# A two-layer hybrid block on one core: the second layer's input projection as seven half-size products, with keys, values and gates formed beside the query up-projection

## The chip, the cores and the metric

The kernel runs on one core of one Trainium2 chip, as one launch. The metric is the device time of that launch in microseconds (us); a time is the median of several runs, and runs of one kernel agree within a few tenths of a per cent. TensorE multiplies matrices out of SBUF into PSUM (eight banks), VectorE (DVE) and ScalarE (ACT) read PSUM and SBUF, GpSimd (POOL) works on SBUF alone, and SyncE (SP) mostly issues transfers. Each engine works through its own queue in order.

## The reference, cut to what matters

Two layers work on 2048 tokens (`x`) and 256 context tokens (`ctx`), all with 1024 channels. Each layer normalises and modulates the tokens, multiplies them by an input matrix, mixes, and multiplies by an output matrix. The second layer is the odd mixer:

```
h = rms_norm(x, pre_norm_w) * (1 + sc_x) + sh_x        # h_c likewise from ctx
ckv, kr, mk, mv, mg, cq, mq, mo, z = split_cols(h @ w_in, O_COLS)   # 1024 x 3632
parts_c = split_cols(h_c @ w_in[:, :O_CTX_COLS], O_COLS[:5])        # first 1072 columns
k_x, v_x = mla_keys_values(ckv, kr, ...)      # rms_norm(ckv) @ w_ukv (256 x 1024), rope
q_x = mla_queries(cq, ...)                    # rms_norm(cq) @ w_uq  (768 x 768), rope
c_out = dense_attention_blocks(q_x, [k_c, k_x], [v_c, v_x])
m_out = readout of two mLSTM passes over mq, mk, mv with gates mg
out = (concat(c_out, m_out) * silu(z)) @ w_out
```

All is float32. The kernel keeps that precision by splitting every matmul operand into a rounded part `hi` and a rest `lo` and adding three products: hi·hi, hi·lo, lo·hi.

## The kernel before

The work is written with a tile framework: the program gives operations in an order, the framework allots buffers from pools, orders each engine's queue (mainly by the program's order, but an operation whose inputs are not ready can be passed by a later one), and inserts the waits. A pool's `bufs` is the number of buffers of a tag; a new tile waits until an old one of the tag is free.

There are 18 token tiles of 128; 0 and 1 are the context. Layer 0 ends with its output projection (`out_proj`), which writes the new tokens to `x1_d` in DRAM. Then comes `layer1_in`, which is what the change rewrites. It handles the tokens in three blocks of six tiles:

- `hT_steps` brings a block's tokens in: per pair of tiles a step `norm` loads the rows (L204), squares and sums them on ACT (L207), gets the factor on POOL (L192, L193) and scales on DVE (L209). Four steps `tr` transpose two chunks of 128 channels each on TensorE, apply the modulation on ACT into `hf` (L226) and split on DVE into `hi` (L228) and `lo` (L229).
- `load_w` brings in some 264 or 256 columns of the weight matrix (L252) and splits them: `whi` on ACT (L255), `wlo` half on POOL and half on DVE (L256).
- `block(b, hi, lo)` runs over the columns. Token-major columns (all but `mq` and `z`) take the tokens as stationary operand and up to 264 weight columns as moving one, 24 matmuls (8 channel chunks x 3) into one PSUM bank `acc`, which DVE (L780) or ACT (L783, Sigmoid) reads. Context tiles leave out the columns past 1072. Feature-major columns (`mq`, `z`) take weights as stationary and 384 tokens (512 in block 0) as moving operand; ACT reads the bank (L799, L803). The results go by SP to `p1_d`, `mo_d`, `mqT_d` and `zT_d` in DRAM.
- `alongside` and `run_part` spread other steps over the steps of `block`: over block 0 the tokens of block 1, over block 1 those of block 2.
- Block 2 has two companions. Over its first 54 steps run `kv_steps`: load and normalise `ckv` (L860, L862), rotate the key part, transpose (`tpc`), split (L832, L833), value and key products (`accv`, `acck`, tag `kacc`, two banks) and their stores. Over the next 20 steps run `gates`, which turns the gate columns into the decay tables of the mLSTM with long scans on DVE (L1275, L1279), and the early steps of `uq_steps` (the query weights).

Then `up` runs the rest of `uq_steps`: per tile load and normalise `cq` (L973), transpose, split `cqh`/`cql`, the rotary product `accr` and the other product `accn` (tag `O`, two banks), and stores. The attention follows.

## Time and profile before

| what | value |
|---|---|
| runs | 3470.11, 3472.04, 3472.26 us (median 3472.04) |
| profiled execution, first to last instruction | 3470.3 us |
| mean granted TensorE clock | 0.985 |
| projection of layer 1, first to last `acc` matmul | 1279 to 2042 us |
| query up-projection after it | to some 2172 us |

The results list no separate time for the profiled execution beside its span. The page gives the busy time of each engine; a weight load (PEld) overlaps the matmul before it, and the end of a matmul is modelled, so the busy time of single matmuls overlaps. In groups of instructions the columns are line, engine, operation, output and inputs, shape and count, then busy time and the mean of one in ns, then the idle time of the engine just before them and what ended it. A row of the waits reads: who, for whom, us in total, times, longest. A row of the timeline or of the chain begins with the time from the start of the span and the duration. A row of the stretches names busy time and (x) the number of instructions per engine, then the granted clock, the share of DMA and GB/s.

### The profile page before, as it was taken

To read this page: it belongs to the slowest core of one execution; us is meant where nothing else is said; L and a number is where in the kernel's file an instruction comes from. 1 tells how busy PE (TensorE), PEld (TensorE's weight loads), DVE (VectorE), ACT (ScalarE), POOL (GpSimd) and SP (SyncE) were. 2 spreads that over 40 slices of the span, in tenths; PEclk is the share of its full clock that TensorE was granted. 3 is DMA by queue.
4 is the path that set the end of the run, shared out by engine and by line. 5 is a ranking of instruction groups with operands and counts; after the bars stand their busy time and mean duration, and the time that the engine had idled before them with its cause. 6 is when DMAs were issued, how large, how long until landed. Compare 5 with 4: busy or idle time off the path is not lost.

```text
span 3470.3 us, 57718 instructions
## 1 busy us (share of the span) xinstructions
PE 3385.0 (98%) x21756; PEld 2976.4 (86%) x21756; DVE 1966.5 (57%) x3550; ACT 1692.7 (49%) x3559; POOL 1193.9 (34%) x1451
## 2 busy tenths in 40 slices
PE   7999999999999989999999999999999999998999
PEld 5989999987888869899999989788888888886776
DVE  4443443337777753333243434788888888875555
ACT  4222221136666652312222333677777777776554
POOL 3324133234333331211232234544444444454221
PEclk9999999999999989999999999999999999998999
DMA  7334223442222143434355555451222122015563
GB/s 264 111 107 127 73 79 118 128 139 85 69 83 72 56 150 125 155 121 131 104 168 162 167 155 155 135 101 36 50 62 49 35 51 62 22 34 151 176 179 97
DMA packets 331895, 376.99 MB, mean 109 GB/s; under 512 B 20205, under 2 KB 284441, under 8 KB 327705
## 3 DMA queue, kind: packets, MB, share of 16 engines
q1 hardware_dynamic: 319312, 315.83, 29.8%
q0 software_dynamic: 11888, 56.92, 6.3%
q8 instruction: 172, 2.82, 0.3%
q14 instruction: 107, 0.87, 0.1%
q10 hardware_dynamic: 416, 0.56, 0.1%
HBM read 267.47 MB, written 105.77 MB: 108 GB/s over the span
## 4 chain that ended last, share of the span: by engine, by line
PE 44%; DVE 2%; DMA 1%; issue 1%; ACT 1%; POOL 1%; SPq 0%; DVEq 0%; POOLq 0%; ACTq 0%
PE S L40 12%; PE O L40 8%; PE T L50 7%; PE acc L40 5%; PE Y L40 5%; PE accn L40 2%; PE pa L40 1%; PE pb L40 1%; PE accr L40 1%; PE acck L40 1%; PE accv L40 1%; DMA cq<-p_d 0%; PE cps L40 0%; PE st L40 0%; DVE mx L1099 0%
## 5 line engine op out<-in xcount | busy, mean ns | idle before, releaser
L40 PE MATMUL acc<-h,whi 128*128 128x384 f32 (+2 forms) x2720 | 708.9, 344 | 3.2 <-ACT whi L255 2.2
L40 PE MATMUL acc<-whi,h 128*128 128x256 f32 (+2 forms) x3328 | 618.1, 285 | 0.0
L40 PEld LDWEIGHTS acc<-whi,h 128*128 128x128 f32 x3328 | 522.4, 190 | 5.6 <-issue 3.5
L40 PEld LDWEIGHTS acc<-h,whi 128*128 128x128 f32 x2720 | 487.4, 190 | 43.0 <-issue 6.0
L40 PE MATMUL S<-kt,qt 96*128 96x512 f32 (+1 forms) x2304 | 494.1, 343 | 2.6 <-ACT P L1101 2.3
L1119 POOL TENSOR_SCALAR P<-P,fa 128x768 f32<-128x768 f32 x384 | 340.2, 905 | 431.9 <-ACT ph L1137 372.7
L40 PEld LDWEIGHTS S<-kt,qt 96*128 96x128 f32 x2304 | 400.6, 189 | 91.7 <-ACT P L1101 17.5
L1138 DVE TENSOR_TENSOR pl<-T,ph 128x512 fp32r<-128x512 f32 x576 | 396.1, 688 | 140.5 <-ACT ph L1137 136.8
L40 PE MATMUL acc<-wlo,h 128*128 128x264 f32 (+1 forms) x1664 | 471.3, 283 | 0.4 <-POOL wlo L256 0.4
L40 PE MATMUL acc<-h,wlo 128*128 128x384 f32 (+2 forms) x1360 | 464.4, 342 | 0.6 <-POOL wlo L256 0.4
L1137 ACT ACTIVATE ph<-T 128x512 fp32r<-128x512 f32 x576 | 342.0, 595 | 163.6 <-PE T L50 156.6
L256 POOL TENSOR_TENSOR wlo<-wraw,whi 128x1024 fp32r<-128x1024 f32 (+2 forms) x86 | 204.3, 2375 | 613.2 <-ACT whi L255 597.0
L1099 DVE TENSOR_REDUCE mx<-S 128x1 f32<-128x768 f32 x384 | 365.6, 952 | 42.5 <-PE S L40 29.3
L1101 ACT ACTIVATE P<-S,mx 128x768 f32<-128x768 f32 x384 | 346.0, 901 | 37.6 <-DVE mx L1099 19.3
L255 ACT ACTIVATE whi<-wraw 128x1024 fp32r<-128x1024 f32 (+2 forms) x172 | 168.0, 1009 | 398.5 <-PE acc L40 213.8
L50 PE MATMUL T<-ident,P 128*128 128x128 f32 x2304 | 348.9, 273 | 5.0 <-DVE pl L1138 3.1
L40 PEld LDWEIGHTS acc<-wlo,h 128*128 128x128 f32 x1664 | 316.7, 190 | 1.5 <-POOL wlo L256 0.8
L50 PEld LDWEIGHTS T<-ident,P 128*128 128x128 f32 x2304 | 275.1, 141 | 42.7 <-DVE pl L1138 7.4
L40 PE MATMUL O<-ph,vh 128*128 128x512 f32 x576 | 267.7, 465 | 0.3 <-ACT ph L1137 0.3
L40 PEld LDWEIGHTS acc<-h,wlo 128*128 128x128 f32 x1360 | 257.7, 189 | 11.1 <-POOL wlo L256 0.7
L40 PE MATMUL O<-pl,vh 128*128 128x512 f32 x576 | 238.9, 415 | 0.4 <-DVE pl L1138 0.2
L256 DVE TENSOR_TENSOR wlo<-wraw,whi 128x1024 fp32r<-128x1024 f32 (+2 forms) x86 | 169.5, 1971 | 111.4 <-ACT whi L255 104.9
(406 smaller groups left out, 5783.1 us busy)
## 6 DMA issues: line engine op xcount, KB each, us to landing
wraw<-in_e_w_in_dram SPq DMA_DIRECT2D x48, 512.0 KB, 4.1
mw<-in_mod_w_dram SPq DMA_DIRECT2D x40, 512.0 KB, 3.9
wraw<-in_o_w_in_dram SPq DMA_DIRECT2D x19, 1024.0 KB, 5.2
wraw<-in_o_w_in_dram SPq DMA_DIRECT2D x18, 1056.0 KB, 7.0
wraw<-in_e_w_in_dram SPq DMA_DIRECT2D x15, 1024.0 KB, 5.4
p_d<-o SPq DMA_DIRECT2D x104, 132.0 KB, 2.2
x_d<-y SPq DMA_DIRECT2D x18, 512.0 KB, 2.8
hx<-x_d SPq DMA_DIRECT2D x18, 512.0 KB, 4.1
```

What stands on the lines that cost most here:

```text
L40: T.matmul(o, l, r, start=start, stop=stop)
L50: T.matmul(o, src, idn, is_transpose=True, start=True, stop=True)
L255: A.activation(hi[:, k : k + 4, :n], raw[:, k : k + 4, :n], AF.Copy)
L256: (V if k else G).tensor_sub(lo[:, k : k + 4, :n], raw[:, k : k + 4, :n], f32(hi[:, k : k + 4, :n]))
L1099: V.tensor_reduce(mx, ps, AX.X, ALU.max, negate=True)
L1101: A.activation(P, ps, AF.Exp, bias=mx, accum_out=st["den"][:, j, i : i + 1])
L1119: G.tensor_scalar(P, P, fa[:, j, i : i + 1], 1.0, op0=ALU.mult, op1=ALU.mult)
L1137: A.activation(ph, tp, AF.Copy)
L1138: V.tensor_sub(pl, tp, f32(ph))
```

## The change

The input projection of layer 1 is computed by Winograd's form of Strassen's scheme. For each block the six token tiles are two halves of three tiles (A1, A2), the 1024 channels two halves of four chunks, and the weight columns of a chunk two halves. Seven products of half the tokens, half the channels and half the columns, each again in three terms of hi and lo, replace eight:

- A sums on POOL (`hW_parts`): of the staged tokens `a11, a12, a21, a22` the operands are a11, a12, s1-a11, s1, a12-(s1-a11), a11-a21, a22, with s1 = a21+a22; all seven are split and kept for the whole block.
- B sums on POOL (`wW_parts`): four subtractions for each chunk, and seven splits (hi on ACT, lo now always on DVE), two products ahead of their use.
- The products are added up in PSUM where two follow one another on the same bank (products 1, 4 and 6 continue 0, 3 and 5), and in SBUF by ACT (product 0) and DVE (products 2 to 6).
- The tokens are first staged in float32 (`hW_stage`, two row buffers `hx` in place of four, no split), since the sums need whole blocks; block b+1 is staged beside block b, and its operands are formed in the last chunk of block b.
- Chunks are now 2 x 268, 2 x 320 (token-major), 2 x 128 and 2 x 256 (feature-major) columns, the four PSUM banks `acc` become six, and context columns reach exactly to 1072.
- `kv_steps` and `gates` leave block 2 (only the key weights and two loads stay there). They now run in `up`, merged with the first 40 and the next steps of `uq_steps`, and share the banks `T` and `O` with it.

The rest of the diff takes out comments. Its core:

```diff
+    def hW_stage(l, tiles, stg, xsrc, xp, pp, nx):
+        st = {}
+        def norm(a):
...
+        def tr(a, k):
+            def f():
+                js = [1 if t < 2 else 0 for t in tiles[a : a + 2]]
...
+                for kk in range(2):
+                    d = k + kk
+                    for i, n in ((0, 2),) if js[0] == js[1] else ((0, 1), (1, 1)):
+                        A.activation(stg[:, d, (a + i) * 128 : (a + i + n) * 128], tp[:, kk, i * 128 : (i + n) * 128],
+                                     AF.Identity, bias=B_col[l][:, d, js[i] : js[i] + 1],
+                                     scale=A_col[l][:, d, js[i] : js[i] + 1])
+            return f
...
+    def hW_parts(stg, T, hp, xp):
+        a11, a12 = (stg[:, k : k + 4, :T] for k in (0, 4))
+        a21, a22 = (stg[:, k : k + 4, T:] for k in (0, 4))
+        ops, st = {}, {}
+        two = lambda ap, j: ap[:, 2 * j : 2 * j + 2, :]
...
+                src = (a11, a12, a11, None, a12, a21, a22)[i]
+                for j in range(2):
+                    if i == 2:
+                        s1 = xp.tile([128, 2, 384], F32, tag="hs1", name="hs1", bufs=1)[:, :, :T]
+                        G.tensor_add(s1, two(a21, j), two(a22, j))
+                        G.tensor_sub(two(a21, j), two(a11, j), two(a21, j))
+                        G.tensor_sub(two(a11, j), s1, two(a11, j))
+                        split(*(two(o, j) for o in ops[3]), s1, V)
+                    if i == 4:
+                        G.tensor_sub(two(a12, j), two(a12, j), two(a11, j))
+                    split(*(two(o, j) for o in ops[i]), two(src, j), V)
...
+    def wW_parts(wsrc, halves, n, wp, wmax):
...
+        def part(i):
+            def f():
+                (b11, b21), (b12, b22) = ((raw[j][:, :4, :n], raw[j][:, 4:, :n]) for j in range(2))
+                hi, lo = ops[i] = [wp.tile([128, 4, wmax], F32R, tag=t, name=t, bufs=3)[:, :, :n] for t in ("whi", "wlo")]
+                if i == 2:
+                    st[0], st[1] = (wp.tile([128, 4, wmax], F32, tag="wt", name="wt", bufs=2)[:, :, :n] for _ in range(2))
+                    G.tensor_sub(st[0], b12, b11)
+                    G.tensor_sub(st[1], b22, st[0])
+                if i == 5:
+                    G.tensor_sub(b12, b22, b12)
+                if i == 6:
+                    G.tensor_sub(b21, b21, st[1])
+                split(hi, lo, (b11, b21, st.get(1), st.get(0), b22, b12, b21)[i], V)
+            return f
...
+    def mmW(ps, lhs, rhs, start):
+        for k in range(4):
+            for a, (i, j) in enumerate(((0, 0), (0, 1), (1, 0))):
+                T.matmul(ps, lhs(i, k), rhs(j, k), start=start and k == 0 and a == 0, stop=k == 3 and a == 2,
+                         skip_group_check=True)
...
     def layer1_in(ue):
...
+            halves = [([2, 3, 0], [4, 5, 1]), ([6, 7, 8], [9, 10, 11]), ([12, 13, 14], [15, 16, 17])]
+            chunks = [
+                ([[(0, 268)], [(268, 268)]], True, True),
+                ([[(536, 268)], [(804, 268)]], True, True),
+                ([[(1072, 320)], [(1392, 320)]], True, False),
+                ([[(1712, 128), (2096, 192)], [(2288, 320)]], True, False),
+                ([[(1840, 128)], [(1968, 128)]], False, False),
+                ([[(2608, 256)], [(2864, 256)]], False, False),
+                ([[(3120, 256)], [(3376, 256)]], False, False),
+            ]
...
+                    if more:
+                        start((c + 1) % len(chunks))
+                    lat = 2 if b == 0 else 3
+                    N = n if tm else lat * 128
+                    subs = (3 if both else lat) if tm else n // 128
...
+                    for i in range(NP):
+                        if i + 2 < NP:
+                            parts[i + 2]()
+                            if i + 2 == NP - 1 and more:
+                                ahead[0][1][1]()
+                        elif more:
+                            ahead[0][2][i + 2 - NP]()
+                        h, w = hops[i], wops[i]
+                        for u in range(subs):
+                            us = slice(u * 128, (u + 1) * 128)
+                            cont = i in (1, 4, 6)
+                            if not cont:
+                                ps[u] = pp.tile([128, 512], F32, tag="acc", name="acc", bufs=6)[:, :N]
...
+                            mmW(ps[u], *((hs, ws) if tm else (ws, hs)), not cont)
+                            if i == 0:
+                                m[u] = op.tile([128, 384], F32, tag="m", name="m", bufs=3)[:, :N]
+                                A.activation(m[u], ps[u], AF.Copy)
+                            elif i == 1:
+                                store(new(), *args(0, 0), ps=ps[u])
+                            elif i == 2:
+                                V.tensor_tensor(m[u], ps[u], m[u], op=ALU.add)
+                            elif i == 3:
+                                o22[u] = op.tile([128, 384], F32, tag="v", name="v", bufs=3)
+                                V.tensor_tensor(o22[u][:, :N], ps[u], m[u], op=ALU.add)
...
+                            yield
+                        if nxt and last and i:
+                            nxt[i - 1]()
...
+                alongside(block(0, h0, mk), flat(steps), 85)
+                steps, h2, mk = stage(2)
+                alongside(block(1, h1, mk), flat(steps), 95)
+            gen = block(2, h2, None)
...
+            first, kv = kv_steps(kw, xk)
+            run_part(gen, 119, [lambda: None] * 8 + first)
+            drain(gen)
...
     def up(ue, ks, xk, kv):
...
+        early, pools, us = uq_steps(uw, xk, uc)
...
+        M = 40
+        merge(kv(kp, pp), [lambda: None] * 4 + early + us[:M])
+        ks.close()
         ha = hd_a.enter_context(tc.tile_pool(name="d_a", bufs=1, **tl))
+        first, ld = load_head(0, ha)
+        n = len(ld) - 6
+        with tc.tile_pool(name="u_g", bufs=1, **tl) as q:
+            merge(steps_of(gates(q, pp), 24), us[M:-24])
+        for o, i in ld[:n]:
+            G.dma_start(o, i)
```

More of the change, by code (lines that the diff above doesn't have):

```diff
@@ new lines, in hW_parts, with new, f @@
+    def hW_parts(stg, T, hp, xp):
[3 more added lines that the diff above has]
+        two = lambda ap, j: ap[:, 2 * j : 2 * j + 2, :]
+        def new(i):
+            ops[i] = [hp.tile([128, 4, T], F32R, tag=f"h{i}{j}", name=f"h{i}{j}", bufs=1) for j in range(2)]
+        def part(i):
+            def f():
+                if i == 2:
+                    new(2)
+                    new(3)
+                elif i != 3:
+                    new(i)
+                if i == 3:
+                    return
+                src = (a11, a12, a11, None, a12, a21, a22)[i]
[9 more added lines that the diff above has]
+                    split(*(two(o, j) for o in ops[i]), two(src, j), V)
+            return f
+        return ops, [part(i) for i in range(NP)]
@@ new lines, in layer1_in, with start, block @@
+            ahead = []
+            def start(c):
+                cols = chunks[c][0]
+                ahead.append(wW_parts(w_in, cols, sum(m for _, m in cols[0]), wp, WM))
+                ahead[-1][1][0]()
+            def block(b, hops, nxt):
+                for c, (cols, tm, both) in enumerate(chunks):
+                    wops, loads, parts = ahead.pop(0)
+                    n = sum(m for _, m in cols[0])
+                    last = c == len(chunks) - 1
+                    more = not (last and b == 2)
+                    if b == 0 and c == 0:
+                        loads[1]()
+                        parts[0]()
+                        parts[1]()
+                    if more:
[3 more added lines that the diff above has]
+                    subs = (3 if both else lat) if tm else n // 128
+                    m = [None] * subs
+                    ps = [None] * subs
+                    o22 = [None] * subs
+                    new = lambda: op.tile([128, 384], F32, tag="o", name="o", bufs=3)
+                    for i in range(NP):
[11 more added lines that the diff above has]
+                                ps[u] = pp.tile([128, 512], F32, tag="acc", name="acc", bufs=6)[:, :N]
+                            hs = lambda j, k: h[j][:, k, us] if tm else h[j][:, k, :N]
+                            ws = lambda j, k: w[j][:, k, :n] if tm else w[j][:, k, us]
+                            mmW(ps[u], *((hs, ws) if tm else (ws, hs)), not cont)
+                            args = lambda half, q: (b, half, u, cols[q], tm, None, N)
+                            if i == 0:
[8 more added lines that the diff above has]
+                                V.tensor_tensor(o22[u][:, :N], ps[u], m[u], op=ALU.add)
+                            elif i == 4:
+                                o = new()
+                                V.tensor_tensor(o[:, :N], ps[u], m[u], op=ALU.add)
+                                store(o, *args(0, 1))
+                            elif i == 5:
+                                V.tensor_tensor(o22[u][:, :N], ps[u], o22[u][:, :N], op=ALU.add)
+                                store(o22[u], *args(1, 1))
+                            else:
+                                o = new()
+                                V.tensor_tensor(o[:, :N], ps[u], m[u], op=ALU.add)
+                                store(o, *args(1, 0))
@@ new lines, in block, with stage @@
+                        if nxt and last and i == NP - 1:
+                            nxt[i]()
+            with ExitStack() as xs:
+                xp = xs.enter_context(tc.tile_pool(name="c_x", bufs=1, **tl))
+                sg = xs.enter_context(tc.tile_pool(name="c_s", bufs=1, **tl))
+                def stage(b):
+                    stg = sg.tile([128, KD, NB * 128], F32, tag="stg", name="stg")
+                    tiles = halves[b][0] + halves[b][1]
+                    return hW_stage(1, tiles, stg, xsrc1, xp, pp, 2), *hW_parts(stg, 384, hp, xp)
+                steps, h0, mk = stage(0)
+                start(0)
+                for n, ts in steps:
+                    n()
+                    for f in ts:
+                        f()
+                for f in mk:
+                    f()
+                flat = lambda st: [f for n, ts in st for f in [n] + ts]
+                steps, h1, mk = stage(1)
+                alongside(block(0, h0, mk), flat(steps), 85)
+                steps, h2, mk = stage(2)
+                alongside(block(1, h1, mk), flat(steps), 95)
@@ L1264, in to_rows @@
             n = min(4, NT - t0)
-            tp = pp.tile([R, 512], F32, tag="kacc", name="gt", bufs=2)
+            tp = pp.tile([R, 512], F32, tag="O", name="gt", bufs=2)
             for i in range(n):
```

213 lines of the change are left out of this document (107 added, 106 removed).

## The prediction

> **What bounds the kernel now.** I read the page first, then the busy time by stretches, then the chain of waits and the timeline inside the second layer's projection.
>
> ```profile
> span 3470.3 us, 57718 instructions
> ...
> PE 3385.0 (98%) x21756; PEld 2976.4 (86%) x21756; DVE 1966.5 (57%) x3550; ACT 1692.7 (49%) x3559; POOL 1193.9 (34%) x1451
> ```
>
> TensorE is busy 98% of the span, and no other engine comes near. The stretches say whether that also holds where the change works: 1230 to 1282 us is the passage into layer 1, to 1762 come blocks 0 and 1 and the start of block 2, to 2045 block 2 with keys, values and gates in it, and to 2172 the query up-projection.
>
> ```profile
> 1230.00:1282.00 52.00, 38.35 (x162) 28.49 (x163) 25.48 (x53) 27.44 (x51) 17.92 (x26) 0.81 0.47 169
> 1282.00:1762.00 480.00, 480.00 (x3528) 468.66 (x3528) 164.19 (x279) 134.80 (x217) 101.46 (x82) 0.99 0.41 132
> 2045.00:2172.00 127.00, 119.77 (x994) 117.96 (x994) 57.56 (x140) 41.11 (x90) 64.88 (x108) 0.99 0.57 173
> ...
> 1762.00:2045.00 283.00, 275.24 (x1936) 265.84 (x1935) 117.59 (x244) 90.14 (x185) 63.72 (x89) 0.98 0.54 158
> ```
>
> Columns: length, then busy PE, weight load, DVE, ACT, POOL, then clock and DMA. From 1282 to 1762 TensorE has no idle time, at clock 0.99, with DVE at 34% and POOL at 21%. A matmul taken away here is time taken away, as long as its replacement waits for nobody.
>
> **What a matmul costs.** The chain is the place to read it, because there each piece hands over to the next:
>
> ```profile
> 1835.73 2.92 PE acc L40 x24
> 1838.65 2.85 PE acck L40 x24
> ...
> 1877.34 2.79 PE accv L40 x12
> ...
> 2025.17 16.89 PE acc L40 x96
> ```
>
> 24 matmuls of 264 columns take 2.92 us, so 0.1217 each; acck has 256 columns: 2.85/24 = 0.1188; accv has 512: 2.79/12 = 0.2325; the last row is the 384-column case: 16.89/96 = 0.1759. The widths of the new code lie between 264 and 384, where a column costs (0.1759 - 0.1217)/120 = 0.00045 us: 268 columns 0.1235, 320 columns 0.1470. Both are interpolations. Time goes by columns, hence seven products instead of eight pay in full.
>
> **What forming an operand costs.** Groups (count, busy, mean ns, idle before) and pieces of the timeline:
>
> ```profile
> L256 DVE TENSOR_TENSOR wlo<-wraw,whi 128x1024 fp32r<-128x1024 f32 x16 | 36.6, 2289 | 55.5 <-ACT whi L255 55.5
> L256 POOL TENSOR_TENSOR wlo<-wraw,whi 128x1024 fp32r<-128x1024 f32 x16 | 39.1, 2446 | 172.2 <-ACT whi L255 171.7 <-PE acc L40 0.4
> L193 POOL TENSOR_TENSOR hr<-hr,half 128x1 f32<-128x1 f32 x18 | 9.9, 548 | 1.4
> L255 ACT ACTIVATE whi<-wraw 128x1024 fp32r<-128x1024 f32 x32 | 32.8, 1053 | 55.6 <-issue 48.5 <-PE acc L40 7.1
> L780 DVE COPY o<-acc 128x264 f32<-128x264 f32 x79 | 33.5, 429 | 109.6 <-PE acc L40 109.6
> ...
> 1279.08 2.43 POOL L256 TENSOR_TENSOR wlo<-wraw,whi 128x1056 fp32r<-128x1056 f32 x1 [3.71 <-DVE h L229]
> 1279.49 2.17 DVE L228 CAST h<-hf 128x256 fp32r<-128x256 f32 x1 [0.47 <-ACT hf L226]
> 1282.03 0.28 DVE L228 CAST h<-hf 128x256 fp32r<-128x256 f32 x1
> 1282.70 1.25 DVE L256 TENSOR_TENSOR wlo<-wraw,whi 128x1056 fp32r<-128x1056 f32 x1
> ```
>
> POOL costs 2.39 ns per element, DVE alone 1.18 (1.25 us for 1056). Beside a POOL pass DVE waits: the CAST of 0.28 took 2.17 and ended with the POOL pass, and wlo on DVE averages 2.29. ACT takes 1.05 us for the same pass, and a read of a 264-column bank 0.43 on DVE.
>
> **Part 1, the matmuls (blocks 0, 1, 2).** Removed, by the loops: 264 columns 576 + 192 + 2 x 864 = 2,496 matmuls, 303.8 us; 256 columns 288 + 2 x 432 = 1,152, 136.9 us; 512 columns 240, 55.8 us; 384 columns 960, 168.9 us; 16 columns 48, at most 5.7 us at the 256-column price (5 taken). Sum 670.4. Added: each product is 4 x 3 matmuls, so a chunk has 84 per sub-tile. 268 columns: 2 chunks x 3 sub-tiles x 84 (504) x 3 blocks = 1,512, 186.7 us; 320 columns: 336 + 2 x 504 = 1,344, 197.6 us; feature-major 256 columns (block 0) 420, 49.9 us, and 384 columns (blocks 1, 2) 840, 147.8 us. Sum 582.0. **-88 us**, on the path. That the count might not fall is no rival: the program fixes it. The transposes are as many as before.
>
> **Part 2, the start of layer 1.** Before, each transposed pair of tiles was split at once, and products could begin on it. Now all six tiles must be staged before the sums of block 0 exist, with two row buffers (hx) instead of four.
>
> ```profile
> 1246.35 0.32 SPq L204 DMA_DIRECT2D hx<-x_d  x1
> 1249.71 1.06 ACT L207 ACTIVATE hjk<-hx 128x1024 bf16<-128x1024 f32 x1 [2.30 <-DMA hx<-x_d]
> 1251.80 0.75 DVE L209 TENSOR_SCALAR hx<-hx,hr 128x1024 f32<-128x1024 f32 x1 [5.48 <-POOL hr L193]
> 1261.12 1.09 PE L50 MATMUL tp<-ident,hx 128*128 128x128 f32 x8 [2.15 <-DVE y L484]
> 1266.46 1.12 PE L50 MATMUL tp<-ident,hx 128*128 128x128 f32 x4 [1.59 <-ACT hf L226]
> 1267.93 1.11 PE L50 MATMUL tp<-ident,hx 128*128 128x128 f32 x4 [0.35 <-ACT hf L226]
> 1279.05 1.25 PE L40 MATMUL acc<-whi,h 128*128 128x264 f32 x4
> ```
>
> A row tile needs 6.2 us from issue to normalised (1246.35 to 1252.55) and the second of a pair about 1.1 more (the ACT pass); a transposing step takes 1.47 us, four per pair. With two buffers a pair cycles in about 4 x 1.3 + 6.2 + 1.1 = 12 us: transposed from 1261, 1273 and 1285, the last ready near 1291. Products 0 and 1 need only the first three tiles and run from about 1280 for 2 x 36 x 0.1235 = 8.9 us. Product 2 needs two chains of three POOL passes over 768 elements, 1.84 us each, so 11 us after 1291 plus a split of 2: about 1305. The gap of 16 us shrinks by the 4.4 us of product 3 if it is queued ahead. **+12**, bounds +5 (the sums overlap the last pair) and +22. The clock in this stretch is 0.81. The Trainium skill (TensorE: Matmul & The Clock Gate, What's actually happening) says that TensorE falls to half clock after an idle window of about 3.4 us and needs as long to recover. The trace agrees in kind; by that rule this stall would cost some 2 us more, 3431 in all.
>
> **Part 3, forming the operands.** The weight bytes stay the same, in less time: DMA 0.41 becomes 0.41 x 670/582 = 0.47, which covers. Count for one block: the half-widths add up to 1,816, so a weight operand has 7,264 elements per partition; DVE splits seven (60 us), POOL sums four (69); the token operands are 14 DVE passes (13) and 8 POOL passes (15) of 768; six row tiles cost DVE 4.5 (0.75 each) and POOL 3.3 (0.55). Taking turns that is 165 us. TensorE's own time is 504 x 0.1235 + 336 x 0.1470 + 420 x 0.1188 = 161.5 us in block 0 and 504 x (0.1235 + 0.1470) + 420 x 0.1759 = 210 us in block 1. So blocks 1 and 2 cover it; block 0 is short by 3.5. The narrow place is its last chunk, which forms block 1's token operands too: 46 us of turns in that chunk and 65 with the next one, against 20 + 31 us of matmuls; 14 short if nothing overlaps, 0 if a third does. **+10** for both together, bounds 0 and +37 (rival B).
>
> **Part 4, banks read in mid-sum.** New in kind: products 1, 4 and 6 add onto the bank of the product before, which ACT (product 0) or DVE (3 and 5) must first have read. That is three waits per chunk, 63 in all, and all that is queued on TensorE stands behind them. With three banks two sub-tiles cover each (2 x 12 x 0.1235 = 3.0 us) against a pass of 0.43 and one queued weight pass of 1.05 to 1.25: no cost. With two banks the cover is 1.4 to 2.1 us: 24 waits, 0.2 us each taken, 5 us. The 128-column chunk has one bank and no cover: 9 waits of 0.43 plus half a queued pass and the hand-over, 1.2 us, 11 us. **+16**. The trace shows no such wait; bounds 0 (another product's matmuls queued in between) and 63 x 0.6 = 38.
>
> **Part 5, keys, values and gates beside the queries.** Their matmuls, DMAs on SP and POOL passes only move. What goes is their cover: between two of them stood 24 acc matmuls (2.92 us). What they now meet is DVE, which the gates hold:
>
> ```profile
> L833 DVE TENSOR_TENSOR kn<-acck,kn 128x512 fp32r<-128x512 f32 x18 | 12.3, 686 | 22.3 <-ACT kn L832 22.3
> L832 ACT ACTIVATE kn<-acck 128x512 fp32r<-128x512 f32 x18 | 10.7, 593 | 22.0 <-PE acck L40 22.0
> L973 DVE TENSOR_SCALAR cq<-cq,ur 128x768 f32<-128x768 f32 x14 | 13.6, 971 | 29.0 <-POOL ur L193 29.0
> ...
> 1986.98 4.95 DVE L1275 TENSOR_TENSOR_SCAN gm<-lfr,lir 4x2304 f32<-4x2304 f32 x1
> 1991.96 5.34 DVE L1279 TENSOR_TENSOR_SCAN gm<-lfr,gm,lir 4x2048 f32<-4x2048 f32 x1
> ...
> PE accr L40 <- ACT cqh L832: 3.9, 1, 3.9
> PE tpr L50 <- POOL qr L273: 1.7, 1, 1.7
> ```
>
> A key or value bank is read in 0.59 + 0.69 = 1.28 us while the other of its two banks fills for 12 x 0.1188 = 1.43: just covered, and late whenever another DVE pass stands ahead. 36 such steps at 0.25 us make 9 us. The scans hold DVE for 10.3 us; block 2 went on through them, because its Silu passes leave by ACT, while the queries need DVE for every tile: about 6 us of that shows. Against it stand the waits of today's stretch (3.9 + 1.7 and smaller ones, some 8 us), which key and value products can now fill. **+7**, bounds -8 (no new wait) and +35 (a cq pass of 0.97 us ahead of each of the 36). On SP the key and value stores come behind the query loads, nobody in this stretch reads them; on POOL the loads of the first head follow the gates, still 24 query steps ahead of the attention.
>
> **Sum.** -88 + 12 + 10 + 16 + 7 = -43 us. The span of the profiled execution is 3470.3 us, inside the runs of 3470.11 to 3472.26 and 1.7 under their median of 3472.04, so nothing of weight lies around it, and the sum is applied to the median: **3429 us**. What a measurement can tell from no change is 0.2%, 7 us: 3465 to 3479 is the same.
>
> **Rivals.**
>
> A, *the gain arrives almost whole*. If the order on the queues puts other products into every wait, only the start's lower bound stays: 3472 - 88 + 5 = 3389. For it: no waits at all between 1282 and 1762, though DVE and POOL split weights there all the time. Against it: that stretch needs 34% + 21% of the two, the new block 0 needs all of them.
>
> B, *forming operands bounds block 0*. If, besides taking turns on SBUF operands, DVE finds no POOL pass under which to hide its reads of PSUM, block 0 takes 165 us plus 15 sub-tiles x 5 reads x 0.43 = 32, so 198 instead of 161.5: 37 us in place of part 3's 10, 3456. For it: the CAST stuck for 2.17 us, with the next DVE pass behind it. Against it: from 1282 to 1762 DVE read 79 banks at a mean of 0.43 us while POOL was busy a fifth of the time, so reads of PSUM seem not to be held up. The Trainium skill (SBUF - State Buffer, Who interferes with whom) has this as a rule: DVE with two SBUF inputs, or in a two-port mode, and GpSimd share one port pair, and the second waits out the whole instruction of the first, while a DVE pass with one SBUF input at most does not take part. The rows agree with the first half; by its second half the reads of PSUM go on beside POOL, which gives 165 us in block 0, the lower price of part 3.
>
> C, *slower: the read-out queue of the query stretch*. Keys, values and queries share two banks (tag O), and each of 36 + 32 steps must be read by ACT and DVE before the next but one may start. With one cq pass (0.97 us) ahead of every read-out, TensorE loses 68 x 0.97 = 66 us in place of 7: 3472 - 88 + 38 + 66 = 3488. It decides from 50/68 = 0.74 us lost per step on. Against it: DVE was busy 57.6 of 127 us with the queries alone, and they lost only some 8 us with the same two banks.
>
> **Chances.** Forecast (about 3395 to 3450) 0.50, A 0.20, B 0.17, C 0.08, and 0.05 for B with half of C, near 3470. So faster 0.87 (the first three), same 0.05, slower 0.08. The range leaves out C and the 0.05, and reaches past A by the two us of its rounding: 3387 to 3463.
>
> **What the new profile would show.** Right: 4,116 acc matmuls in place of 4,896, at 0.1235 and 0.147 us each; blocks 1 and 2 near 210 us apiece with TensorE idle under 5%; the largest idle piece at the first block's third product, behind the POOL sums; idle pieces of about a microsecond behind ACT and DVE in the 128-column chunk and in block 0; wlo on DVE again over 2 us beside POOL. Wrong: acc pieces longer per column than 0.00046 us; block 0 near 200 us (B); the stretch from the end of block 2 to the attention well over 127 + 57 us, the kv matmuls being 108 x 0.2325 + 216 x 0.1188 + 6 for transposes (C); or the first product starting after 1290.

## The result and the profile after

The changed kernel takes **3513.45 us** (median of 4 runs, 3510.40 to 3516.82) against 3472.15 for the kernel before in the same session: ratio 1.0116, 95% interval 1.0102 to 1.0131. It is 1.2% slower; forecast were 3429 us and a gain. The head of the page after:

```profile
span 3515.0 us, 56792 instructions
...
PE 3345.3 (95%) x20976; PEld 2931.4 (83%) x20976; DVE 2183.9 (62%) x3671; ACT 1816.7 (52%) x3750; POOL 1380.0 (39%) x1512
```

TensorE has 780 matmuls fewer (21756 to 20976), and its share of the span fell from 98% to 95%. The stretches of the profile after (columns as before: length, PE, weight load, DVE, ACT, POOL, clock, DMA):

```profile
1282.00:1341.00 59.00, 41.70 (x274) 40.07 (x275) 43.20 (x39) 31.56 (x55) 34.68 (x21) 0.76 0.29 94
1341.00:1440.00 99.00, 96.47 (x712) 95.08 (x711) 63.33 (x72) 51.65 (x79) 43.53 (x22) 1.00 0.46 144
1440.00:1502.00 62.00, 48.46 (x343) 47.21 (x343) 47.10 (x42) 31.10 (x48) 44.42 (x18) 0.86 0.44 135
1502.00:1707.00 205.00, 193.02 (x1311) 191.22 (x1310) 117.23 (x131) 84.88 (x131) 80.66 (x40) 0.97 0.39 120
1707.00:1748.00 41.00, 32.16 (x170) 31.07 (x169) 33.10 (x30) 20.52 (x30) 26.03 (x11) 0.88 0.31 93
1748.00:1964.00 216.00, 210.98 (x1430) 209.28 (x1429) 119.41 (x148) 80.90 (x123) 79.32 (x41) 1.00 0.37 115
1964.00:2208.00 244.00, 208.36 (x1456) 188.44 (x1455) 142.24 (x356) 90.84 (x218) 104.99 (x190) 0.91 0.68 201
```

Block 2 (1748 to 1964) runs nearly as forecast, at 216 us for 210. The first chunk of the layer (1282 to 1341), the end of block 0 (1440 to 1502) and the end of block 1 (1707 to 1748) do not: TensorE idles, and the granted clock is only 0.76, 0.86 and 0.88 there. The rest of block 1 (1502 to 1707) has 12 us of idle time, and the whole query stretch (1964 to 2208) has 36, at clock 0.91.

Where the 44.7 us between the two profiled executions (3515.0 and 3470.3) came from, by the times of the first and last instruction of each part:

| part | before | after | difference |
|---|---|---|---|
| first `acc` of layer 1 at | 1279.1 | 1282.2 | +3.2 |
| first to last `acc` | 762.6 | 681.6 | -81.0 |
| last `acc` to the attention's first product with the values | 180.0 | 303.4 | +123.4 |
| rest of the program | 1248.7 | 1247.8 | -0.9 |

The matmuls of keys, values and gates, 64 us at the undisturbed price of each, left the second row and joined the third. Besides, the second row should have lost 88. So the projection lost 71 us to waits and a slower clock (-81 + 64 + 88), and the third row 59 (123 - 64). Some 52 of these 59 lie between the last `acc` and the last `accn` of the queries. The rest lies in the attention's first products behind it, from 2208.6 to 2267.2; experiment 7, whose work there is the same, took 53.1 us for that piece instead of 58.6, so most of that rest belongs to this one execution and not to the change.

What TensorE waited for in the projection (after; who, for whom, us in total, times, longest):

```profile
PE acc L361 <- ACT h L1020: 15.8, 3, 7.9
PE acc L361 <- DVE v L976: 14.4, 5, 5.5
PE acc L361 <- DVE wlo L1021: 9.3, 4, 5.5
PE acc L361 <- ACT m L963: 7.2, 5, 3.6
PE acc L361 <- DVE v L970: 6.9, 4, 2.4
PE acc L361 <- ACT whi L1020: 4.0, 1, 4.0
...
```

Some 29 us are operands not yet formed (`h`, `wlo`, `whi`), 28.5 are banks that products 1, 4 and 6 continue and nobody had read yet (`v`, `m`). They are few waits, and long: up to 5.5 us for a read of 0.43. The timeline of after shows how one comes about (at 1563), and two other places that matter below (1300 and 2111):

```profile
1300.48 7.37 DVE L1021 TENSOR_TENSOR h<-stg,h 128x768 fp32r<-128x768 f32 x3
1302.12 2.41 POOL L320 TENSOR_TENSOR stg<-stg 128x768 f32<-128x768 f32 x1
1302.97 0.59 PE L361 MATMUL acc<-whi,h 128*128 128x268 f32 x1 [7.85 <-ACT h L1020]
...
1312.91 0.60 PE L361 MATMUL acc<-whi,h 128*128 128x268 f32 x1 [5.57 <-ACT h L1020]
...
1316.73 0.94 ACT L963 ACTIVATE m<-acc 128x268 f32<-128x268 f32 x3
...
1563.81 2.96 POOL L346 TENSOR_TENSOR wt<-wraw 128x1280 f32<-128x1280 f32 x1 [20.10 <-DVE o L973]
1566.85 4.09 POOL L347 TENSOR_TENSOR wt<-wraw,wt 128x1280 f32<-128x1280 f32 x1
1570.89 2.90 POOL L349 TENSOR_TENSOR wraw<-wraw 128x1280 f32<-128x1280 f32 x1
1574.74 0.75 DVE L266 TENSOR_SCALAR hx<-hx,hr 128x1024 f32<-128x1024 f32 x1 [5.93 <-POOL hr L193]
1576.51 0.75 DVE L266 TENSOR_SCALAR hx<-hx,hr 128x1024 f32<-128x1024 f32 x1 [1.02 <-POOL hr L193]
1577.17 0.43 DVE L976 TENSOR_TENSOR v<-acc,v 128x268 f32<-128x268 f32 x1
1577.66 0.59 PE L361 MATMUL acc<-whi,h 128*128 128x268 f32 x1 [5.47 <-DVE v L976]
...
2111.07 0.84 ACT L1171 ACTIVATE jk<-cq 128x768 bf16<-128x768 f32 x1 [9.47 <-DMA cq<-p_d]
2112.93 0.58 ACT L1227 ACTIVATE qn<-accn 128x512 fp32r<-128x512 f32 x1
2113.53 0.69 DVE L1228 SCALAR_TENSOR_TENSOR qn<-accn,qn 128x512 fp32r<-128x512 f32 x1 [2.45 <-ACT qn L1227]
2114.28 1.89 PE L50 MATMUL gt<-ident,gpad 128*36 128x128 f32 x8 [2.53 <-DVE qn L1228]
```

At 1563 POOL makes three weight sums of 3 to 4 us without a pause. The factor of the norm stands behind them on POOL; DVE waits for the factors with the scaling of two token rows (5.93 and 1.02 us); behind these, on DVE, stands the read of a bank; and behind the read stands TensorE, for 5.47 us. The price goes on after the wait, in the stretches around it:

```profile
1574.00:1576.00 2.00, 0.00 (x0) 0.00 (x0) 0.75 (x1) 0.00 (x0) 0.88 (x4) 1.00 0.00 0
1578.00:1580.00 2.00, 2.00 (x10) 2.00 (x10) 1.69 (x3) 0.00 (x0) 0.92 (x1) 0.50 0.22 69
1580.00:1582.00 2.00, 2.00 (x10) 2.00 (x9) 0.44 (x1) 1.21 (x1) 2.00 (x1) 0.50 0.43 137
1584.00:1588.00 4.00, 4.00 (x31) 4.00 (x30) 0.00 (x0) 1.36 (x4) 0.00 (x0) 1.00 0.02 4
```

For some 6 us TensorE is fully busy at clock 0.50, with 10 matmuls in 2 us where there are 15 or 16 later: another 3 us for a wait of 5.5. The Trainium skill (TensorE: Matmul & The Clock Gate, What's actually happening) has this as half clock after at least one idle window of about 3.4 us and full clock after at least one busy window of that length, the windows running freely. The fall agrees; the clock was at 0.50 from 1576.9 to 1583.7, twice that length, so full clock came back 6 us after TensorE had set in again.

### The profile page after: what moved, and what is told of

It reads as the page before. It is cut to its first block, busy times and chain, and to the rows that moved or that the text cites. A ratio compares the mean times of both kernels' runs of the same rounds, so it can differ in the third digit from the quotient of the medians.

```text
span 3515.0 us, 56792 instructions
## 1 busy us (share of the span) xinstructions
PE 3345.3 (95%) x20976; PEld 2931.4 (83%) x20976; DVE 2183.9 (62%) x3671; ACT 1816.7 (52%) x3750; POOL 1380.0 (39%) x1512
## 4 chain that ended last, share of the span: by engine, by line
PE 42%; DVE 2%; POOL 2%; DMA 2%; issue 2%; ACT 1%; POOLq 0%; DVEq 0%; SPq 0%; ACTq 0%
PE S L40 11%; PE O L40 7%; PE T L50 7%; PE acc L361 5%; PE Y L40 5%; PE accn L40 1%; PE pa L40 1%; PE pb L40 1%; PE accr L40 1%; PE cps L40 1%; PE acck L40 0%; DMA cq<-p_d 0%; PE accv L40 0%; POOL P L1319 0%; DMA wraw<-in_o_w_in_dram 0%
## 5 line engine op out<-in xcount | busy, mean ns | idle before, releaser
L40 PE MATMUL acc<-h,whi 128*128 128x384 f32 (+2 forms) x1920 | 492.8, 340 | 1.3 <-DVE h L228 1.2
L361 PE MATMUL acc<-whi,h 128*128 128x268 f32 (+1 forms) x1904 | 403.4, 305 | 33.6 <-ACT h L1020 15.8
L40 PEld LDWEIGHTS acc<-h,whi 128*128 128x128 f32 x1920 | 341.2, 190 | 33.5 <-issue 6.0
L361 PEld LDWEIGHTS acc<-whi,h 128*128 128x128 f32 x1904 | 318.1, 194 | 37.2 <-ACT h L1020 16.8
L40 PE MATMUL acc<-h,wlo 128*128 128x384 f32 (+1 forms) x960 | 323.7, 337 | 0.0
L361 PE MATMUL acc<-wlo,h 128*128 128x268 f32 (+1 forms) x952 | 287.8, 303 | 2.3 <-DVE wlo L1021 2.3
L361 PE MATMUL acc<-h,whi 128*128 128x384 f32 (+1 forms) x840 | 202.7, 330 | 16.9 <-DVE v L976 8.7
L1021 DVE TENSOR_TENSOR wlo<-wraw,whi 128x1072 fp32r<-128x1072 f32 (+3 forms) x105 | 166.9, 1592 | 79.5 <-ACT whi L1020 79.4
L751 POOL TENSOR_SCALAR P<-P,den 128x640 f32<-128x640 f32 (+2 forms) x144 | 110.1, 766 | 245.5 <-DVE den L750 226.0
L1020 ACT ACTIVATE whi<-wraw 128x1072 fp32r<-128x1072 f32 (+3 forms) x105 | 112.2, 1071 | 160.2 <-PE acc L361 106.3
```

What stands on the lines that cost most here:

```text
L40: T.matmul(o, l, r, start=start, stop=stop)
L361: T.matmul(ps, lhs(i, k), rhs(j, k), start=start and k == 0 and a == 0, stop=k == 3 and a == 2, skip_group_check=True)
L751: G.tensor_scalar(pt[:, 1 : nk + 1], pt[:, 1 : nk + 1], den, 1.0, op0=ALU.mult, op1=ALU.mult)
L1020: A.activation(hi, src, AF.Copy)
L1021: (eng or G).tensor_sub(lo, src, f32(hi))
```

## The experiments

All times are medians; the changed kernel is 3513.45, the kernel before 3471.9 to 3475.1 in the sessions below. Except where the text says otherwise, an edit is made to the changed kernel.

**1. The move without the new projection.** The old projection, with keys, values and gates beside the queries as in the changed kernel (and its pools in other places, so that it fits).

```diff
-            halves = [([2, 3, 0], [4, 5, 1]), ([6, 7, 8], [9, 10, 11]), ([12, 13, 14], [15, 16, 17])]
...
+            def block(b, hi, lo):
...
+                        mm3(ps[:, :m], [(hi[:, k, sl], lo[:, k, sl], whi[:, k, :m], wlo[:, k, :m]) for k in range(KD)])
...
-            run_part(gen, 119, [lambda: None] * 8 + first)
+            run_part(last, 74, [lambda: None] * 8 + first)
```

> The projection as before (eight products, same banks, same splits), but keys, values and gates run beside the query up-projection, as in the changed kernel. Theory 1 (the move costs by itself: the cover of the 24-matmul pieces is gone and TensorE waits for read-outs by ACT and DVE): the stretch from the last projection matmul to the first attention output loses the same 50 us or so that it loses in the changed kernel, so about 3472 + 50 = 3522, at least 3510. Rival (the move is free, and the loss after the projection only follows from the new projection ending ragged): within 7 us of before.

3505.02, ratio 1.0094 (1.0072 to 1.0115): **the move costs 33 us** in all. The stretch from the last `acc` to the attention is 48 us longer than before plus the moved 64, about as the theory had it. But 16 come back ahead of it, which the theory had left out, so that the total lies below its range and far above the rival's: the first `acc` comes 6 us earlier (1273.0 in place of 1279.1), and the old projection without company hardly waits (busy time of TensorE 687 of 689 us):

```profile
1273.00:1962.00 689.00, 687.20 (x5020) 674.98 (x5021) 207.76 (x316) 177.38 (x274) 126.93 (x86) 0.99 0.38 121
```

The new projection lasts 682 us, starts 9 us later and ends at 1964.2, 2.4 us later than this one. So nothing of the 88 us arrives: against the old projection alone, 81 of them are lost between the first and the last `acc`, and the rest by the later start. (The 71 further up are counted against the old projection with its company, which takes 10 us longer than it would alone.)

**2. No sums.** All additions and subtractions of tokens and weights on POOL are left out; the products use the pieces as they are.

```diff
-                    G.tensor_sub(st[0], b12, b11)
-                    G.tensor_sub(st[1], b22, st[0])
...
+                    st[0], st[1] = b12, b22
```

> The changed kernel without its sums on GpSimd: all ten sums of tokens and weights per block and chunk are left out, and the splits take unsummed parts, so the same matmuls, splits and read-outs run on other numbers. Theory 1 (the projection waits because the POOL sums hold up DVE, and with it everything queued behind): of the 88 us that TensorE waits or runs slow between the first and last projection matmul over 60 go, time about 3513 - 60 = 3453. Rival (the banks that are read in mid-sum cost by themselves, whatever POOL does): under 15 us go, time 3500 or more.

3448.05, ratio 0.9926 (0.9900 to 0.9953): 65 us less, as theory 1 had it. First to last `acc` falls by 60 us to 622; from there to the last `accn` it takes 244 us as in the changed kernel. The sums are most of the projection's loss of 71.

**3. No bank read in mid-sum.** Each bank is read only when its products are through; the terms that need an earlier reading are left out.

```diff
-                            if i == 0:
-                                m[u] = op.tile([128, 384], F32, tag="m", name="m", bufs=3)[:, :N]
-                                A.activation(m[u], ps[u], AF.Copy)
...
```

> The changed kernel with no bank read in mid-sum: the copies after products 0, 3 and 5 are left out, each bank is read when both products are in it, so the results lack some terms; one ACT and one DVE pass less per sub-tile. Theory 1 (a bank read is late only because the queue is): the waits turn into waits for operands, 10 to 25 us go, time about 3495. Rival (mid-sum reads are the cause): the 28 us of waits on them and the slow clock after them go, 45 us or more, time 3468 or less.

3485.51, ratio 1.0037 (1.0023 to 1.0051): 28 us less, a little over the 10 to 25 of theory 1 and far under the 45 of the rival. The waits that go are partly replaced by waits for operands:

```profile
PE acc L361 <- DVE wlo L1016: 26.0, 13, 5.1
PE acc L361 <- ACT h L1015: 12.3, 3, 5.4
```

In the changed kernel `wlo` had 9.3. Whoever is late on DVE stops TensorE, at this place or at the next.

**4. No factor behind the sums.** The tokens are scaled by a constant instead of the norm's factor, so that DVE's scaling waits for nothing on POOL.

```diff
-                    r = rstd_of(xp, ms, 1, 1.0 / D, "hr")
+                    r = half
```

> The changed kernel, but the staging of the tokens scales by a constant instead of the norm's factor, so that the two small POOL passes per tile are left out and the scaling on DVE no longer waits for POOL. Theory 1, in the part that a small pass stands behind 10 us of sums on POOL while DVE's queue waits for it: 10 to 25 us go, about 3495. Rival (order on POOL does not matter, DVE is simply full): within 5 us of the changed kernel.

3505.69, ratio 1.0092 (1.0066 to 1.0119): 8 us, between the rival's 5 and the 10 that the theory wanted at least. The chain at 1563 is real, but it is a small part.

**5. The sums on DVE.**

```diff
-                    G.tensor_sub(st[0], b12, b11)
-                    G.tensor_sub(st[1], b22, st[0])
+                    V.tensor_sub(st[0], b12, b11)
+                    V.tensor_sub(st[1], b22, st[0])
```

and so for the other six lines.

> All sums of tokens and weights go to DVE instead of POOL; nothing else changes. Per block DVE gains the 69 us of weight sums and 15 us of token sums at POOL's price, half of that (about 42 us) at its own 1.18 ns per element. Theory 1 (POOL's long sums, and the port that DVE gives up to them, delay the norm's factor, the splits and the reads of banks behind them): most of what leaving the sums out gave (65 us) comes back, since DVE has room in blocks 1 and 2: 3513 - 40 = 3473, between 3463 and 3485. Rival (the number of elementwise passes is what counts, on whichever engine; DVE becomes the queue that everything stands behind): no gain, 3505 to 3530.

3461.91, ratio 0.9968 (0.9956 to 0.9980): 51.5 us less than the changed kernel, more than expected, and **faster than the kernel before**. The queue that became longer got faster. The groups say why; after first, then this kernel, then the one without sums (count, busy us, mean ns, idle before):

```profile
L1021 DVE TENSOR_TENSOR wlo<-wt,whi 128x1024 fp32r<-128x1024 f32 x12 | 28.2, 2377 | 19.9 <-ACT whi L1020 19.9
L967 DVE TENSOR_TENSOR m<-acc,m 128x320 f32<-128x320 f32 x16 | 7.7, 488 | 5.1 <-PE acc L361 5.1
L347 POOL TENSOR_TENSOR wt<-wraw,wt 128x1280 f32<-128x1280 f32 x6 | 23.5, 3922 | 0.5
```

```profile
L1021 DVE TENSOR_TENSOR wlo<-wt,whi 128x1024 fp32r<-128x1024 f32 x12 | 14.5, 1222 | 6.8 <-ACT whi L1020 6.7
L347 DVE TENSOR_TENSOR wt<-wraw,wt 128x1280 f32<-128x1280 f32 x6 | 8.9, 1482 | 0.0
L967 DVE TENSOR_TENSOR m<-acc,m 128x320 f32<-128x320 f32 x16 | 7.7, 488 | 5.0 <-PE acc L361 5.0
```

The same split takes 2377 ns beside POOL's sums and 1222 without them; a sum takes 3922 ns on POOL and 1482 on DVE. This split is the one that suffers most; the 30 splits of 1024 elements that read `wraw` go from 1223 to 1675 ns. A read of a bank takes 488 in both: a pass with one input out of PSUM was not lengthened, it only stands behind passes that are. And the projections as one stretch each, of after, of this kernel and of the one without sums:

```profile
1282.00:1964.00 682.00, 622.77 (x4229) 613.92 (x4230) 423.37 (x457) 300.62 (x462) 308.64 (x150) 0.95 0.38 119
```

```profile
1281.00:1912.00 631.00, 607.64 (x4227) 601.59 (x4227) 438.69 (x561) 300.62 (x461) 30.88 (x44) 0.98 0.42 129
```

```profile
1281.00:1903.00 622.00, 603.81 (x4227) 599.32 (x4228) 333.61 (x457) 300.69 (x462) 24.73 (x44) 0.98 0.42 131
```

With the same 457 instructions DVE is busy 423 us beside POOL's sums and 334 without. So handing the sums to POOL makes DVE's own passes 90 us longer, which are waits in turns with POOL, and doing the 104 sums of this stretch itself costs it 105 (439 - 334). POOL took only 15 us off DVE, and added 284 us of long passes.

**6. A bank for each product**, what was continued in PSUM now added in SBUF by DVE.

```diff
-                            cont = i in (1, 4, 6)
+                            cont = False
...
-                                store(new(), *args(0, 0), ps=ps[u])
+                                o = new()
+                                V.tensor_tensor(o[:, :N], ps[u], m[u], op=ALU.add)
+                                store(o, *args(0, 0))
```

> Every product gets a bank of its own; what products 1, 4 and 6 added onto the bank of the product before is now added in SBUF by DVE (one more pass per sub-tile). Leaving out the mid-sum reads with their terms gave 28 us. Theory 1 (the wait on a read in mid-sum is what costs): 3513 - 22 = 3491, between 3485 and 3498. Rival (the waits were only the place where lateness of DVE shows, and an extra DVE pass makes it later): 3508 to 3525.

3492.13, ratio 1.0056 (1.0041 to 1.0071): 21 us less, as the theory had it.

**7. Keys and values on other banks.**

```diff
-                ps = pp.tile([128, 512], F32, tag="O", name="accv", bufs=2)
+                ps = pp.tile([128, 768], F32, tag="S", name="accv", bufs=2)[:, :512]
```

> Key and value products use the two banks of tag S, idle until the attention, instead of sharing the two of tag O with the query products; the rest is as in the changed kernel. Rival C of the prediction (two banks shared by keys, values and queries hold the query stretch up): the stretch from the last acc to the first attention product loses 15 us or more, total 3490 to 3500. Theory 2 (the stretch is held up by the chain of small passes on ACT, DVE and POOL, and by the clock falling after each gap; banks are not short): within 6 us of the changed kernel, 3507 to 3515.

3511.98, ratio 1.0115 (1.0100 to 1.0130): nothing. That keys and values share banks with the queries costs nothing that can be measured here.

**8. Sums on DVE and a bank for each product**, edits 5 and 6 together.

> Sums on DVE and a bank for each product together. If the two costs are separate, the gains add: 3513 - 40 - 22 = 3451, between 3440 and 3465, which would be below the kernel before (3472). If they are two faces of one lateness of DVE, the pair gives hardly more than the sums alone, 3470 to 3485; and if DVE itself becomes the bound in block 0, more than 3490.

3455.82, ratio 0.9950 (0.9934 to 0.9967). Within what "separate costs" expected, but 6 us under the sums alone and not 21: with the sums on DVE, TensorE waits 6.5 us for banks read in mid-sum (`v`, `m`) in place of 28.5, so most of these waits have gone already.

**9. Only the gates moved**, in the kernel before; keys and values stay beside block 2.

```diff
-                run_part(last, 20, merged([lambda: None] * 2 + steps_of(gates(q, pp), 24), [lambda: None] * 4 + early))
+            run_part(last, 20, [lambda: None] * 4 + early)
...
+            merge(steps_of(gates(q, pp), 24), us[-68:-24])
```

> The kernel before with its own projection; of what moves, only the gates go beside the query products (in the same places of the query list as in the changed kernel), keys and values stay beside the last block of the projection. Moving all three cost 33 us. Theory 1 (the gates are the larger half: their setup and scans come in a burst on DVE while the query products need DVE for every tile): +20 against the kernel before, 3492, between 3486 and 3500. Rival (keys and values are what the queries cannot cover): +8 or less, 3472 to 3480.

3494.07, ratio 1.0063 (1.0045 to 1.0081) to 3475.06: 19 us for the gates alone, of 33 for the whole move.

**10. Gates, keys and values on banks of their own**, on top of 8.

```diff
-            tp = pp.tile([R, 512], F32, tag="O", name="gt", bufs=2)
+            tp = pp.tile([128, 768], F32, tag="S", name="gt", bufs=2)[:R, :512]
```

and so for `gbp`, `gq`, `accv`, `acck`.

> The version with sums on DVE and a bank for each product (3456), and key, value and gate products on the two double banks of tag S, idle until the attention. If the gates' transposes are held up by sharing two banks with the query products: 8 us or more are gained, 3440 to 3448. If the passes of DVE and ACT are the limit there, as for keys and values: within 5 us of 3456.

**3435.96**, ratio 0.9891 (0.9876 to 0.9905): 20 us less than 8, more than the 8 to 16 expected, and 1.1% below the kernel before. It is the fastest of all that were run.

**11. All three spread evenly** over the query steps, on top of 10.

```diff
-        M = 40
-        merge(kv(kp, pp), [lambda: None] * 4 + early + us[:M])
+            merge(kv(kp, pp), [lambda: None] * 4 + early + us[:-24], [lambda: None] * 12 + steps_of(gates(q, pp), 24))
```

> As the run before, and keys, values and gates are spread evenly over all but the last 24 query steps, in one merged order, instead of keys and values over the first 40 and gates over the next 44. The work is the same. Theory 1 (bursts of small passes, gates' setup above all, find no products ahead of them): half of the 50 us over the matmuls' own time in this stretch go, 3425 to 3440. Rival (the chain load, norm, transpose, split, product, read-out is as long wherever it stands; spreading only makes the gates end later, in front of the mLSTM): 3448 to 3465.

3445.44, ratio 0.9915 (0.9900 to 0.9929): 9 us slower than 10. That is in neither range, but on the rival's side, and the theory falls: spreading these steps evenly gains nothing. Other orders were not tried.

**12. Sums that nobody reads.** POOL makes as many sums as long as before, into scratch tiles.

```diff
-                    G.tensor_sub(b12, b22, b12)
+                    G.tensor_sub(st[0], b22, b12)
...
-                split(hi, lo, (b11, b21, st.get(1), st.get(0), b22, b12, b21)[i], V)
+                split(hi, lo, (b11, b21, b22, b12, b22, b12, b21)[i], V)
```

> The changed kernel with all sums still done on POOL, as many and as long, but into scratch tiles that nobody reads; the splits take tokens and weights as they are. So POOL's time and its turns with DVE stay, and the wait of the operands for their sums goes (the output is another one). Leaving the sums out gave 65 us. Theory 1 (turns with DVE, and what stands behind the sums on POOL's queue, are most of the cost): most of it stays, 3490 to 3510. Rival (operands that wait for their sums are most of it): 3450 to 3465.

3512.92, ratio 1.0111 (1.0091 to 1.0131): no gain at all over the changed kernel. That no operand waits for its sum any more is worth nothing as long as POOL does the sums; their presence on POOL is worth all of the 65 us. DVE's 457 instructions take 414 us, nearly as long as in the changed kernel:

```profile
1280.00:1966.00 686.00, 620.79 (x4228) 613.26 (x4228) 413.77 (x457) 300.28 (x461) 318.51 (x150) 0.95 0.38 118
```

With experiment 4 (8 us stand behind the sums on POOL's own queue) the turns with DVE remain as the main cause. That POOL's sums hold the weight buffers longer is not it: in neither of the two profiles does a split of these weights wait for a load.

**13. Only the gates on banks of their own**, in the changed kernel (the edit of 10 for `gbp`, `gt` and `gq` alone).

> The changed kernel, with nothing else altered than the gates' transposes and sums on the two double banks of tag S instead of the two of tag O that the query products use. Theory 1 (gates waiting in the same two banks hold the queries up, whatever stands in the projection): 15 to 22 us less than the changed kernel, 3491 to 3499. Rival (the 20 us came from keys and values on banks of their own, once DVE had been relieved of the banks read in mid-sum, or from both together): 3507 or more.

3495.34, ratio 1.0066 (1.0049 to 1.0083): 18 us less. That the gates share two banks with the query products costs 18 to 20 us, with or without a mended projection. The same 73 us, of after and of this kernel:

```profile
2089.00:2162.00 73.00, 56.47 (x379) 49.22 (x377) 49.25 (x101) 20.51 (x42) 29.78 (x42) 0.81 0.52 137
```

```profile
2089.00:2162.00 73.00, 62.54 (x499) 60.27 (x498) 53.81 (x115) 25.03 (x53) 37.06 (x54) 0.93 0.64 169
```

499 matmuls instead of 379, at clock 0.93 instead of 0.81. The rows at 2111 above show one way in which it costs: ACT waits 9.47 us for a load of `cq`; behind that wait on ACT stands the read of a query bank; the gates' transposes want one of the same two banks, and TensorE stands behind them for 2.53 us. How much of the 18 us goes this way was not measured.

The new projection with keys, values and gates left beside block 2 was not run.

## Why the prediction was wrong

**Part 1 held.** 780 matmuls are gone, and the undisturbed price is as interpolated: the 320-column chunk of block 2, 252 products at 0.147 us, was forecast at 37.0 us and took

```profile
1814.90:1851.90 37.00, 37.00 (x255) 37.00 (x254) 18.99 (x22) 11.32 (x13) 16.60 (x6) 1.00 0.32 102
```

The 88 us are real, but no version collects them all: experiment 8's projection lasts 627 us from first to last `acc`, against 689 for the old one without company (experiment 1), so 62 of them.

**Part 2 had the mechanism and half the size.** Product 2 was forecast for 1305 and began at 1302.97, but that agreement is partly luck. It began with the first half of its operand only; the second half came at 1312.91, after another wait of 5.57 us. Product 1, which the sum lets run before it, came behind it: it continues on the banks of product 0, and ACT read those only at 1316.73, behind the splits that wait for POOL's sums. Giving product 1 banks of its own (experiment 6) lets it run at once, and then product 2 waits for the same reads by ACT; the first chunk is as long, 59.7 us against 59.1. The sum priced a POOL pass at 1.84 us and a split at its time alone; here POOL and DVE take turns (sums of 2.4 us, three splits in 7.37 us at 1300, 0.95 each when alone). It also took 1.3 us for a transposing step where its own row has 1.47. And TensorE ran at half clock through these waits until past 1316. In all the first chunk and the later beginning cost 28 us (25 over the matmuls' price, 3 before it), not 12, and more than the bound of 22.

**Part 3 is the step that failed in the projection: "So blocks 1 and 2 cover it".** It added up the turns of a block and compared the sum with the block's matmuls. TensorE does not wait for sums over a block; it waits whenever a pass that it needs next stands in a queue behind a long one. Block 1 had 210 us of products by the prediction's own sum and lasted 246; block 0 had 161.5 and lasted 220, and half of that difference lies in the first chunk. Experiments 2, 5 and 12 show the turns as the cause: without the sums block 1 lasts 215 us, with the sums on DVE 217, with unread sums on POOL 241. Rival B had the turns, but looked for them in block 0 alone and blamed reads of PSUM. Those were not stretched, as the row with 488 ns in both kernels shows, and as the rule of the Trainium skill (SBUF - State Buffer, Who interferes with whom) that the prediction quoted would have it.

**Part 4 had the mechanism, the size was off:** 16 forecast, 21 gained by giving each product its bank, 28 by leaving the readings out. It was not many waits of 0.2 us but 14 of up to 5.5. And they are hardly a cost of their own: experiment 8 gained only 6 by the same edit once the sums were on DVE.

**Part 5 is the largest miss: +7 forecast, +59 measured, of which 52 up to the last query product.** Of the 88 us by which the parts of the profile exceed the forecast (84 in the medians), this part makes up 52 (59 - 7), part 2 16 (28 - 12), and parts 3 and 4 together 20 (46 measured, 26 forecast). Two things were overlooked. First, the sum costed the gates by their scans on DVE, at 6 us; what costs most is that they share two banks with the query products (18 us, experiment 13). In the place shown at 2111, ACT, held by a load, stands in front of them. The scans (`gm`) stop TensorE for 1.0 us in the changed kernel, and for 4.4 once the gates have banks of their own. The table of waits before showed next to no wait for the gates' steps (`gt`, `gbp`), but beside block 2 they had two banks (`kacc`) that the projection did not use. These are two rows of before, one of after and two of experiment 13:

```profile
PE gt L50 <- DVE gbt L1256: 1.2, 1, 1.2
PE gbp L40 <- DVE lf L1247: 0.2, 1, 0.2
...
PE gq L50 <- DVE gm L1479: 1.0, 1, 1.0
...
PE gq L50 <- DVE gm L1477: 2.3, 1, 2.3
PE gq L50 <- DVE gm L1479: 2.1, 1, 2.1
```

Rival C had the right two banks, but put keys and values into them; experiment 7 found no effect there. Second, where keys and values begin, there are no query products yet:

```profile
1964.00:2017.00 53.00, 38.51 (x200) 31.80 (x199) 31.63 (x90) 25.13 (x68) 22.02 (x46) 0.84 0.78 241
```

In these first 53 us TensorE does 200 matmuls, 40 of them transposes, and the first query product starts at 2005. How much this start costs was not measured alone, so that part of the cause stays open: keys and values on top of the gates cost 14 us (33 - 19) in the total, and no edit here got it back.

**The clock is what makes the small terms large.** The prediction gave it 2 us, in one place. In the changed kernel TensorE stands idle for 59 us of the projection and is busy for 46 at half clock, which loses 23 more; in the query stretch up to the last `accn` it is 36 and 18. Before, the projection had 8 us of idle time and 10 lost at half clock.

**No rival had the result.** C ended highest, at 3488, with one part bad and the others as forecast. What happened is that parts 2 to 5 together were far too low, because each was costed as if the engines met the added work evenly. Two of the prediction's own signs of being wrong did show: block 0 near 200 us (it lasted 220), and the stretch behind block 2 well over 127 + 57 us (244 up to the last `accn`).

## What to carry to other kernels

Where TensorE is busy 98% of the time, a change that takes matmuls away and adds passes on other engines is worth only what the waits for these passes leave of it. The passes must be followed queue by queue, the longest pass and what stands behind it first, not as sums of busy time over a block. Before handing elementwise work with two SBUF inputs to POOL, compare the time that it takes off DVE with the time that DVE then waits in turns: here 105 against 90 us. When steps are moved beside other work, look at what they share there, banks above all, and at which engine's next instruction waits for a load.

## What the runs showed of the hardware that was not expected

- POOL's sums of two SBUF operands cost DVE nearly as much time as making them itself (90 and 105 us for 104 passes), while taking 2.6 times as long (3922 against 1482 ns for 1280 elements beside DVE's splits). DVE's reads of a PSUM bank with one input from SBUF were not lengthened at all (488 ns in both cases).
- After a wait of 5.5 us TensorE ran at clock 0.50 for about 6 us of full work, so that the wait cost about 3 us more.
- A longer queue on one engine was faster than two that take turns: DVE busy for 439 of 631 us fed TensorE better than DVE busy for 423 of 682 with POOL's help.
